# Low parts of weights in three stages of a two-block transformer: every subtraction on VectorE instead of every second one on GpSimd

## Chip, cores and metric

One NeuronCore of a Trainium2 chip runs the whole program. The metric is device time in microseconds (us). Engines carry the names of the profile: PE is TensorE's matmul, PEld its weight load, DVE is VectorE, ACT is ScalarE, POOL is GpSimd, SP is SyncE, which issues most of the DMAs.

## What is computed

Two blocks of two layers each, in float32, on 512 tokens of width 1024, and 256 context tokens in the second block. The second block is the one that the change touches:

```python
for i in range(DEPTH):                                   # second_block
    hx = rmsnorm(x, norm_g[i, 0]) * (1.0 + sc_x) + sh_x
    hc = rmsnorm(ctx, norm_g[i, 0]) * (1.0 + sc_c) + sh_c
    if i % N_MIXERS == 0:
        yx = conv_module(hx, *cp)                        # and yc for ctx
    else:
        yx, yc = attention_module(hx, hc, ...)           # 16 heads of 64, 4 key heads
    x = x + g_x * rmsnorm(yx, norm_g[i, 1])
    fx = rmsnorm(x, norm_g[i, 2]) * (1.0 + scf_x) + shf_x
    x = x + gf_x * rmsnorm(swiglu(fx, ffn_w1[i], ffn_w3[i], ffn_w2[i]), norm_g[i, 3])
    # the same for ctx where i < DEPTH - 1

def conv_module(h, ...):
    a, gt = jnp.split(h @ w_pw1 + b_pw1, 2, axis=-1)
    u = a * jax.nn.sigmoid(gt)
    u = depthwise_conv(u, w_dw) + b_dw                   # 31 taps
    return jax.nn.silu(layernorm(u, ln_g, ln_b)) @ w_pw2 + b_pw2
```

## The kernel before, in words

Every matrix product runs in three passes, so that float32 weights and activations keep their precision: each operand is split into a high part (rounded to the matmul's format) and a low part (what is left), and PE adds high x high, high x low and low x high (`dense`, L184 to L186; `dense_tok`, L192 to L194). Activations are split where they are made (L269, L270, L282, L284, L285). Weights come from memory in float32, chunk by chunk, and are split on the fly by `Core.weights`: SP loads a chunk of at most 128x1024 into `raw`, ACT casts it into `whi` (L165), and DVE or POOL subtracts, `wlo = raw - whi` (L168). `raw`, `whi` and `wlo` have three buffers each. Which engine subtracts is set by one number, `core.lo_pool`: 0 means always DVE, 2 means that every second chunk (by a running count) goes to POOL, 1 means always POOL. The two lines that say so:

```python
eng = nc.gpsimd if self.lo_pool and self.chunks % self.lo_pool == 0 else nc.vector
eng.tensor_tensor(lo[:, :n], raw[:, :n], hi[:, :n], op=ALU.subtract)
```

The program sets that number stage by stage. In the second block: `conv_layer` takes `CONV_LO` (2) for the products of the gated unit (`glu`, 32 chunks) and for the second product on the context (`back(T)`, 8 chunks); `ffn2` takes 2 in its first and its last part, which this text calls the edges of the feed-forward, and 0 between; `attention_layer` takes `PROJ_LO` (2) for the queries', keys' and values' projections (`project`, 28 chunks); the attention's output product uses 1, then `LO_O` (2), and is not touched. The first block has settings of its own, not touched either.

Around these products the engines have other work. In the convolution, DVE runs the 31 taps over the context, one instruction per tap (L929, tile `yc`), as side work behind the gated unit; POOL builds tap weights (L936, `wt`) and issues half of the copies of shifted channels (L941, `ug`); PE runs the taps over x (L948, `cv`). At the edges of the feed-forward and after the attention, norms run from one part to the next: sums of squares (L221, `acc`), a column sum on PE (L238), an inverse root by Newton steps on DVE (L204 to L210, `rs_*`), its broadcast on PE (L243), scaling of eight tiles, three of them on ACT and POOL (L258, L259) and five on DVE (L261), the residual sum (L830, three on POOL, five on DVE) and the split (L269, L270). In the projections DVE turns queries and keys (L1082, `rp`), POOL finishes that (L1084, L1085) and subtracts low parts of activations (L1119, L1133, `stk`), and PE transposes them (L1091, `qT`).

The order on each engine is set when the program is built: a scheduler takes ready instructions by their place in the program and by an estimate of their length, and each engine then runs its list strictly in that order. So an instruction that moves to another engine changes the lists of both, and the scheduler rearranges PE's and ACT's too.

Of the kernel before, what the change touches and what calls it, by code (L numbers as in the profile page):

```python
# [17 lines left out]
PSUM = bass.MemoryType.PSUM  # L18
# [10 lines left out]
# ---------------------------------------------------------------- column vectors  # L29
# [38 lines left out]
PROJ_LO = 2  # L68
MM = 4
AT = 4  # L70
CONV_LO = 2
# [15 lines left out]
class Scratch:  # L87
    """[128, 256] tiles that the norms pass through"""
# [8 lines left out]
class Core:  # L97
    """Pools, constants and the pieces that every layer uses."""
# [25 lines left out]
    def issue_behind(self, ins, others):  # L124
        """keep ins behind the others in their engine's queue"""
        for o in others:
            self.tc.add_manual_dep(ins.ins, o.ins.name,
                                   mybir.DependencyInfo(mybir.DependencyClass.NoSync, mybir.DependencyReason.DATA),
                                   reason="activation tables")
        return ins  # L130
# [15 lines left out]
    def side_work(self, n):  # L146
        """up to n steps of work that runs beside the matrix products"""
        for _ in range(n):
            if next(self.side, None) is None:
                return  # L150
# [7 lines left out]
    # ---- weights: raw float32 in, exact hi + lo parts out  # L158
# [12 lines left out]
    def chunk(self, src):  # L171
        """one chunk [128, k, n] of a matrix"""
        _, k, n = src.shape
        hi, lo = self.weights(src.rearrange("p k n -> p (k n)"), k * n)
        return (hi[:, : k * n].rearrange("p (k n) -> p k n", n=n),
                lo[:, : k * n].rearrange("p (k n) -> p k n", n=n))

    def dense(self, out, w, xs, cols=slice(0, S)):
        """out[feature, token] = sum over k of w[k].T @ xs[k], in three exact-product passes"""
        hi, lo = w  # L180
        mm = self.nc.tensor.matmul
        n = len(xs)
        for k, (xh, xl) in enumerate(xs):
            mm(out, lhsT=hi[:, k, :], rhs=xh[:, cols], start=(k == 0), stop=False)  # L184
            mm(out, lhsT=hi[:, k, :], rhs=xl[:, cols], start=False, stop=False)  # L185
            mm(out, lhsT=lo[:, k, :], rhs=xh[:, cols], start=False, stop=(k == n - 1))  # L186

    def dense_tok(self, out, x, cols, w, first, last):
        """out[token, feature] += x.T @ w for one tile of k and 128 tokens"""
        (xh, xl), (wh, wl) = x, w  # L190
        mm = self.nc.tensor.matmul
        mm(out, lhsT=xh[:, cols], rhs=wh, start=first, stop=False)  # L192
        mm(out, lhsT=xh[:, cols], rhs=wl, start=False, stop=False)
        mm(out, lhsT=xl[:, cols], rhs=wh, start=False, stop=last)  # L194

    # ---- rsqrt on a small tile, by Newton steps on the vector engine
# [16 lines left out]
    # ---- norms over the features of a feature-major array  # L213
    def square_sum(self, pool, sums, x, k):
        """the squares of tile k join sums, which ends as two tiles"""
        nc = self.nc
        n = x.shape[-1]
        sq = pool.tile("sqx" if k else "acc")[:, :n]
        nc.scalar.activation(sq, x, AF.Square)
        if 0 < k < KD - 1:  # L220
            nc.vector.tensor_tensor(sums[0], sums[0], sq, op=ALU.add)  # L221
        else:
            sums.append(sq)

    def rstd_psum(self, sums):
        """1 / rms per token on all partitions, in PSUM; and the last step of the rsqrt"""
        nc = self.nc
        n = sums[0].shape[-1]
# [17 lines left out]
    def rstd(self, pool, sums):  # L246
        """the same in PSUM and in SBUF"""
        pb, _ = self.rstd_psum(sums)
        rb = pool.tile("rb")[:, : pb.shape[-1]]
        self.nc.scalar.copy(rb, pb)  # L250
        return pb, rb

    def times_rb(self, pool, x, scale, rb, k):
        """x * rb * scale"""
# [9 lines left out]
    def modulate(self, pool, out, x, scale, shift, rb, k):  # L264
        """out (hi, lo) = x * rb * scale + shift"""
        nc = self.nc
        hi, lo = out
# [4 lines left out]
    def modulated(self, pool, h, xs, cols, scale, shift, sums):  # L272
        """the norm of the tiles xs, scaled and shifted per feature, into the columns of h"""
# [17 lines left out]
    # ---- modulation vectors: w.T tile by tile against rows of the activation, summed on the fly  # L291
    def modulation_rows(self, wt, vecs, bias, dsts, tiles, first=0, pool=None):
        """one step per tile of 128 outputs; wt: [48, 128, 1024]"""
# [21 lines left out]
    def silu_row(self, pool, src, name):  # L315
        """silu of a vector of 1024, on all partitions"""
# [6 lines left out]
    def gains(self, g, mod, slot, name):  # L323
        """g * (1 + mod[slot]) as columns"""
# [5 lines left out]
# ------------------------------------------------------------------------------- first block  # L330
def rope_tables(core, pool, cos, sin):
    """cos and sin of positions * inv_freq, token-major [128, 4, 32]"""
# [26 lines left out]
def rope_gains(core, pool, cos, sin, g, name):  # L359
    """cos and sin with the gains of both halves folded in: [128, 4, 4, 32]"""  # L360
# [9 lines left out]
def mla_latents(core, l, ts):  # L370
    """the products of the latents and of the shared rope key, token-major"""
# [11 lines left out]
def mla_heads(core, tmp, pool, kp, l, ups, cos, sin, rows):  # L383
    """queries, keys and values of all heads; kp holds what the attention reads"""
# [47 lines left out]
    def rope(eng, out, x, tab, shape):  # L432
        """out, x: views [..., 64]; tab: (cos g1, sin g2, cos g2, sin g1) broadcast to the shape"""
# [6 lines left out]
    # queries: token-major, then turned; the rope halves of a pair of heads share a tile of keys,  # L440
    # so each head's queries are zero in the other head's rows
# [34 lines left out]
    # keys and values  # L476
# [42 lines left out]
def mla_attention(core, pool, yp, heads, table):  # L519
    """causal softmax attention; y as hi and lo parts, one pair of tiles per head"""  # L520
# [41 lines left out]
def stick_rows(core, kp, l, which):  # L562
    """queries (which = 0) or keys (1) of the stick-breaking heads, feature-major"""
# [39 lines left out]
def stick_attention(core, pool, yp, heads, table):  # L603
    """a = exp(z + reverse cumulative sum of log(1 - sigmoid z)) over the past keys; keys on partitions"""
# [36 lines left out]
def gate(core, parts, l, br, m):  # L641
    """the argument of a gate's sigmoid, in tiles that hold a part of the tokens each"""
# [11 lines left out]
def gated(core, l, parts, ys, br, m, behind):  # L654
    """sigmoid(g) * (y @ w_branch) for one tile of features, in place of g"""
# [11 lines left out]
def first_layer(core, pool, l, ups, mod, cos, sin, next_mod, early, finish):  # L667
    """the layer's normed input is in core.h already; finish(columns, sums) makes the next one's"""
# [57 lines left out]
    with tc.tile_pool(name=f"ff{l}", reuse_waits="tile", bufs=1) as fp:  # L726
        tails = {}

        def up(i, hl, cols):
            """one tile of the hidden layer; a causal convolution of width 3 sits before the gate"""  # L730
# [57 lines left out]
# ------------------------------------------------------------------------------ second block  # L788
class Base:
    """the tokens of x or of ctx, feature-major: x, the normed input h (hi, lo) and a layer's output y"""  # L790
# [5 lines left out]
class Stream:  # L796
    """some columns of a base that go through a phase together"""
# [23 lines left out]
def post_norm(core, st, gate_slot, ng, squares=True):  # L821
    """x += gate * rmsnorm(y, ng); leaves the sums of squares of the new x"""
# [17 lines left out]
def ffn2(core, fp, i, bases, parts, nbuf, finish):  # L840
    """swiglu as a sequence of steps; parts: (first tile, end, steps up or down of streams that share the
    weights); streams run one after the other hide each other's norms"""
    nc, a = core.nc, core.a
    for part, (k0, k1, steps) in enumerate(parts):
        first, last = part == 0, part == len(parts) - 1
        hid = {b.tag: [core.pair(fp, b.n, "hid" + b.tag, nbuf) for _ in range(k0, k1)] for b in bases}
        core.lo_pool = 2 if first or last else 0
# [38 lines left out]
def conv_layer(core, X, A, B, T, post, pre, between):  # L886
    """conformer convolution module of x (as one stream X, then its halves A and B) and of ctx (T)"""
# [3 lines left out]
    with tc.tile_pool(name="cv_c", reuse_waits="tile", bufs=1, side="right") as cp, ExitStack() as es:  # L891
# [12 lines left out]
        def glu(st, m, u):  # L904
            """u = (h @ w_a + b_a) * sigmoid(h @ w_g + b_g) for one tile of channels, with zeros around"""
# [12 lines left out]
        def taps_dve(us):  # L918
            """the convolution over ctx on the vector engine, one step per tap"""
# [12 lines left out]
        def shifted(m, u):  # L932
            """over x on the tensor engine: four shifted copies of each 32 channels fill the rows of the array"""
# [25 lines left out]
        def layer_norm(st, t):  # L959
            """silu(layernorm) into h; t: the sum of all tiles but the last"""  # L960
# [63 lines left out]
def axial_tables(core, pool):  # L1024
    """cos and sin with the queries' and the keys' gains folded in, and the gains; pool's one tile holds them
    until the attention's probabilities take its place"""
# [16 lines left out]
def attention_layer(core, pool, A, B, T, axial, tables, dense_psum, finish):  # L1043
    """grouped-query attention of x (halves A and B) over x and ctx (T); 16 heads of 64, 4 key heads"""
# [3 lines left out]
    with ExitStack() as es:  # L1048
# [8 lines left out]
        with tc.tile_pool(name="at_t", reuse_waits="tile", bufs=1) as tmp:  # L1057
# [18 lines left out]
            def rope(out, x, tab, t, heads):  # L1076
                """interleaved pairs: out, x [128, heads, 64] views"""
# [9 lines left out]
            def turned(src, dst, act):  # L1087
                """four tiles [128 tokens, 128] turned into dst [128, 4, 128]"""
# [8 lines left out]
            def keys(st, pss):  # L1097
                """for the queries' hi and lo parts stacked on the partitions: each part of the keys twice"""
# [55 lines left out]
        with tc.tile_pool(name="at_p", reuse_waits="tile", bufs=1) as pp, core.psum_pool("ps_a") as pa:  # L1154
            pairs = []

            def scores(u):
                """of 128 queries of a head, and the negated maximum of each"""
# [13 lines left out]
            def exponentials(u, ps, s2, rc):  # L1172
                """turned to put the keys on the partitions"""
# [27 lines left out]
            def output(p, yps):  # L1201
                """divided by the sums of the exponentials, into h"""
# [268 lines left out]
# --------------------------------------------------------------------------------- the host  # L1471
def _mt(w):
    """[..., K, M] -> [..., M / 128, 128, K / 128, 128]: one contiguous chunk per 128 columns"""
# [6 lines left out]
def _kc(w, kk):  # L1480
    """[..., K, N] -> [..., K / (128 kk), 128, kk, N]"""
# [6 lines left out]
def _col(v):  # L1488
    """[..., n * 128] -> [128, prod * n] columns, tile by tile"""
    return v.reshape(-1, P).T  # L1490


def _pairs(a, b):
    """interleave chunk lists along the chunk axis"""
# [78 lines left out]
```

## Time and profile before

| | before |
|---|---|
| time, median of 3 runs | 3262.71 us (3258.6 to 3264.51) |
| span of the profiled execution, first to last instruction | 3256.1 us |
| own time of the profiled execution | not listed apart from its span; the median lies 6.6 us above the span |
| PE busy | 3045.2 us, 94% of the span |
| DVE busy | 2118.7 us, 65% |
| ACT busy | 1378.8 us, 42% |
| POOL busy | 818.3 us, 25% |
| mean granted TensorE clock | 0.972 |
| L168 on POOL | 189 instructions, mean 2472 ns |
| L168 on DVE | 433 instructions, mean 1163 ns |

Busy shares are means over stages with different limits. The convolution lies at about 1562 to 1822 us from the start of the span, the first edge of the feed-forward behind it up to 2000, its middle up to 2400, its last edge to 2500, the projections to 2640, the attention to some 2820, the last feed-forward from 2845 to the end, with edges up to 2905 and from 3190. A stage is best read from a view that gives each engine's busy time in that stretch.

### The profile page before, as it was taken

Reading aid. Unit: us, or ns where it says so; the run is one execution under the profiler, and the core shown is the slowest. Engines: PE = TensorE matmul, PEld = TensorE weight load, DVE = VectorE, ACT = ScalarE, POOL = GpSimd, SP = SyncE. Lnnn points to the kernel's source line nnn. Section 1 sums busy time; section 2 is a strip of 40 time slices with the busy share of each in tenths; the row PEclk is TensorE's granted clock in tenths of the full one; section 3 lists DMA queues with packets and bytes.
Section 4 is the critical chain, followed back from the end, with each engine's and each line's share of the span. In section 5 each row is a group of like instructions: output and inputs, shape, how many; then the busy total and the mean of one; then the engine's idle time right before and its main releaser. Section 6 shows DMA issues by size and latency. Waiting matters only on the chain. (4 is left out here: it accounts for less than half of the span.)

```text
span 3256.1 us, 45125 instructions
## 1 busy us (share of the span) xinstructions
PE 3045.2 (94%) x16916; PEld 2554.5 (78%) x16916; DVE 2118.7 (65%) x3863; ACT 1378.8 (42%) x2523; POOL 818.3 (25%) x618
## 2 busy tenths in 40 slices
PE   6999999999999999999899789999998789999997
PEld 5776888888777787877856589888887667898887
DVE  7654775657543688888997786544549976672326
ACT  4535552335534562324513564222235556553223
POOL 4000223233000222223555352000025621240023
PEclk9999999999999999999999889999999989999998
DMA  6442445654221355554434345333434310243323
GB/s 239 135 138 95 136 168 190 192 179 150 90 72 49 123 174 175 170 188 131 146 111 119 104 136 175 98 110 130 138 106 139 119 44 14 75 143 111 94 97 117
DMA packets 129322, 416.69 MB, mean 128 GB/s; under 512 B 16208, under 2 KB 21840, under 8 KB 129104
## 3 DMA queue, kind: packets, MB, share of 16 engines
q1 hardware_dynamic: 123984, 404.96, 38.5%
q10 hardware_dynamic: 3072, 4.43, 0.5%
q0 software_dynamic: 2048, 4.43, 0.5%
q8 instruction: 133, 2.18, 0.3%
q14 instruction: 85, 0.70, 0.1%
HBM read 402.81 MB, written 2.10 MB: 124 GB/s over the span
## 5 line engine op out<-in xcount | busy, mean ns | idle before, releaser
L165 ACT CAST whi<-raw 128x1024 fp32r<-128x1024 f32 (+4 forms) x622 | 599.0, 966 | 1008.8 <-PE dn L185 299.9
L168 POOL TENSOR_TENSOR wlo<-raw,whi 128x1024 fp32r<-128x1024 f32 (+3 forms) x189 | 467.0, 2472 | 1275.0 <-ACT whi L165 1237.4
L168 DVE TENSOR_TENSOR wlo<-raw,whi 128x1024 fp32r<-128x1024 f32 (+4 forms) x433 | 503.2, 1163 | 284.3 <-ACT whi L165 276.8
L184 PE MATMUL dn<-hi,whi 128*128 128x256 f32 (+1 forms) x1088 | 363.5, 338 | 19.8 <-DVE x L778 13.5
L186 PE MATMUL dn<-hi,wlo 128*128 128x256 f32 (+1 forms) x1088 | 361.5, 336 | 7.6 <-DVE wlo L168 7.5
L185 PE MATMUL dn<-lo,whi 128*128 128x256 f32 (+1 forms) x1088 | 364.5, 336 | 1.7 <-DVE lo L285 1.5
L184 PE MATMUL up<-hh,whi 128*128 128x512 f32 (+1 forms) x800 | 292.1, 367 | 7.2 <-ACT hh L269 7.2
L185 PE MATMUL up<-hl,whi 128*128 128x512 f32 (+1 forms) x800 | 292.5, 366 | 0.3 <-DVE hl L270 0.2
L186 PE MATMUL up<-hh,wlo 128*128 128x512 f32 (+1 forms) x800 | 291.7, 365 | 0.0
L308 DVE SCALAR_TENSOR_TENSOR mjunk<-mraw,crow 128x1024 f32<-128x1024 f32 (+1 forms) x176 | 224.0, 1273 | 39.9 <-PE g L185 21.1
L184 PEld LDWEIGHTS dn<-hi,whi 128*128 128x128 f32 x1088 | 207.3, 191 | 47.9 <-issue 14.0
L186 PEld LDWEIGHTS dn<-hi,wlo 128*128 128x128 f32 x1088 | 206.9, 191 | 32.5 <-DVE wlo L168 9.9
L185 PEld LDWEIGHTS dn<-lo,whi 128*128 128x128 f32 x1088 | 208.8, 192 | 25.0 <-DVE lo L285 2.3
L860 DVE TENSOR_TENSOR s<-s,pv 128x512 f32<-128x512 f32 (+1 forms) x76 | 41.0, 539 | 283.7 <-PE pv L186 278.0
L184 PE MATMUL pa<-hh,whi 128*128 128x512 f32 (+1 forms) x496 | 179.5, 362 | 6.2 <-ACT whi L165 3.4
L185 PE MATMUL pa<-hl,whi 128*128 128x512 f32 (+1 forms) x496 | 178.8, 361 | 2.8 <-DVE hl L270 2.7
L186 PE MATMUL pa<-hh,wlo 128*128 128x512 f32 (+1 forms) x496 | 178.0, 359 | 2.0 <-DVE wlo L168 2.0
L184 PEld LDWEIGHTS up<-hh,whi 128*128 128x128 f32 x800 | 152.4, 191 | 31.4 <-ACT hh L269 7.7
L185 PEld LDWEIGHTS up<-hl,whi 128*128 128x128 f32 x800 | 152.4, 191 | 24.5 <-DVE hl L270 0.8
L186 PEld LDWEIGHTS up<-hh,wlo 128*128 128x128 f32 x800 | 152.3, 191 | 23.8
L186 PE MATMUL pv<-hh,wlo 128*128 128x512 f32 (+1 forms) x432 | 152.7, 353 | 0.2 <-POOL wlo L168 0.2
L184 PE MATMUL pv<-hh,whi 128*128 128x512 f32 (+1 forms) x432 | 152.5, 353 | 0.0
(471 smaller groups left out, 7427.7 us busy)
## 6 DMA issues: line engine op xcount, KB each, us to landing
raw<-in_w SPq DMA_DIRECT2D x148, 512.0 KB, 3.4
raw<-in_w_up SPq DMA_DIRECT2D x100, 512.0 KB, 3.5
mraw<-in_w_modt SPq DMA_DIRECT2D x96, 512.0 KB, 3.6
mraw<-in_w_adat SPq DMA_DIRECT2D x80, 512.0 KB, 3.4
raw<-in_w_pw SPq DMA_DIRECT2D x56, 512.0 KB, 3.5
raw<-in_w_down SPq DMA_DIRECT2D x48, 448.0 KB, 3.5
raw<-in_w_g SPq DMA_DIRECT2D x32, 512.0 KB, 3.2
raw<-in_w_out SPq DMA_DIRECT2D x32, 512.0 KB, 3.6
```

The costliest lines, as they stand in the source:

```text
L165: nc.scalar.copy(hi[:, :n], raw[:, :n])
L168: eng.tensor_tensor(lo[:, :n], raw[:, :n], hi[:, :n], op=ALU.subtract)
L184: mm(out, lhsT=hi[:, k, :], rhs=xh[:, cols], start=(k == 0), stop=False)
L185: mm(out, lhsT=hi[:, k, :], rhs=xl[:, cols], start=False, stop=False)
L186: mm(out, lhsT=lo[:, k, :], rhs=xh[:, cols], start=False, stop=(k == n - 1))
L308: behind(nc.vector.scalar_tensor_tensor(junk, raw, 1.0, v, op0=ALU.mult, op1=ALU.mult, accum_out=d[:, f : f + 1]))
L860: nc.vector.tensor_tensor(s, s, pv, op=ALU.mult)
```

## The change

Three settings go from 2 to 0; `core.chunks` counts on as before. The rest of the diff takes out comments and docstrings.

```diff
-PROJ_LO = 2
+PROJ_LO = 0
 MM = 4
 AT = 4
-CONV_LO = 2
+CONV_LO = 0
...
 def ffn2(core, fp, i, bases, parts, nbuf, finish):
...
-        core.lo_pool = 2 if first or last else 0
+        core.lo_pool = 0
```

Over the program, L168 stands 189 times on POOL and 433 times on DVE before, and 79 and 543 times in the change: 110 subtractions move, 90 of 128x1024, 16 of 128x512 and 4 of 128x768.

POOL's list in the projections, before (`stk` are low parts of queries and keys that PE waits to transpose, `qf` and `kt` turned queries and keys, `ctx` and `hp` the context's norm):

```order
L830 TENSOR_TENSOR ctx_10741<-ctx_10741,hp 128x256
L168 TENSOR_TENSOR wlo<-raw,whi 128x1024
L830 TENSOR_TENSOR ctx_10743<-ctx_10743,hp 128x256
L1084 TENSOR_TENSOR kt_23103<-rp 128x128
L1085 TENSOR_TENSOR kt_23103<-rp 128x128
L168 TENSOR_TENSOR wlo<-raw,whi 128x1024 x2
L1133 TENSOR_TENSOR stk<-qf,stk 128x8x64
```

The same place of POOL's list in the change:

```order
L830 TENSOR_TENSOR ctx_10741<-ctx_10741,hp 128x256
L259 TENSOR_TENSOR hp<-hp,rb 128x256
L830 TENSOR_TENSOR ctx_10743<-ctx_10743,hp 128x256
L1133 TENSOR_TENSOR stk<-qf,stk 128x8x64
L1084 TENSOR_TENSOR kt_23129<-rp 128x128
L1085 TENSOR_TENSOR kt_23129<-rp 128x128
L1133 TENSOR_TENSOR stk<-qf,stk 128x8x64
```

Three subtractions stood between the context's residual sums and the next `stk`; none is left.

DVE's list at the context's residual sums in the same stage (`pg` is a gain, `rs_v` begins the inverse root that waits for the sums `acc`), before:

```order
L830 TENSOR_TENSOR ctx_10740<-ctx_10740,hp 128x256
L830 TENSOR_TENSOR ctx_10742<-ctx_10742,hp 128x256
L168 TENSOR_TENSOR wlo<-raw,whi 128x1024
L261 SCALAR_TENSOR_TENSOR hp<-yc_13721,pg,rb 128x256
L261 SCALAR_TENSOR_TENSOR hp<-yc_13722,pg,rb 128x256
L830 TENSOR_TENSOR ctx_10744<-ctx_10744,hp 128x256
L830 TENSOR_TENSOR ctx_10745<-ctx_10745,hp 128x256
```

And in the change:

```order
L261 SCALAR_TENSOR_TENSOR hp<-yc_13722,pg,rb 128x256
L168 TENSOR_TENSOR wlo<-raw,whi 128x1024
L830 TENSOR_TENSOR ctx_10744<-ctx_10744,hp 128x256
L221 TENSOR_TENSOR acc<-acc,sqx 128x256
L830 TENSOR_TENSOR ctx_10745<-ctx_10745,hp 128x256
L825 TENSOR_TENSOR pg<-mod_105,cols 128x8
L168 TENSOR_TENSOR wlo<-raw,whi 128x1024
L221 TENSOR_TENSOR acc<-acc,sqx 128x256
L168 TENSOR_TENSOR wlo<-raw,whi 128x1024
L221 TENSOR_TENSOR acc<-acc,sqx 128x256 x3
L168 TENSOR_TENSOR wlo<-raw,whi 128x1024 x2
L240 TENSOR_SCALAR rs_v<-rb 128x2
```

From the first of the residual sums (`ctx_10738`) to `rs_v` DVE has three subtractions in its list before and six in the change.

## Rows read from the trace of the kernel before

**Rows 1.** Busy time of each engine by stretch (stretch, its length, engines, PEclk, DMA, GB/s).

```profile
1562.00:1740.00 178.00, 160.05 (x950) 117.69 (x948) 169.87 (x309) 51.52 (x73) 98.36 (x94) 0.94 0.40 121
1740.00:1822.00 82.00, 79.96 (x564) 51.51 (x563) 44.57 (x83) 33.78 (x60) 33.53 (x37) 1.00 0.43 127
1822.00:2000.00 178.00, 145.95 (x1069) 140.87 (x1069) 144.37 (x312) 107.98 (x221) 76.51 (x53) 0.87 0.40 127
2000.00:2400.00 400.00, 400.00 (x2280) 351.02 (x2279) 191.57 (x309) 91.32 (x146) 12.56 (x6) 1.00 0.39 126
2400.00:2500.00 100.00, 89.37 (x599) 81.61 (x598) 75.33 (x149) 48.61 (x100) 42.05 (x32) 0.95 0.37 111
2500.00:2640.00 140.00, 107.88 (x495) 84.49 (x494) 133.31 (x268) 73.03 (x126) 85.36 (x64) 0.90 0.37 122
2845.00:2905.00 60.00, 53.46 (x394) 51.99 (x393) 51.90 (x109) 37.18 (x74) 27.77 (x19) 0.90 0.42 140
2905.00:3190.00 285.00, 285.00 (x1378) 239.48 (x1377) 80.56 (x93) 84.53 (x112) 40.91 (x18) 1.00 0.34 107
3190.00:3257.00 67.00, 47.32 (x390) 46.35 (x388) 46.38 (x82) 22.68 (x37) 27.69 (x19) 0.86 0.38 118
```

**Rows 2.** The same stretches, L168 alone: DVE busy (count), POOL busy (count).

```profile
1562.00:1740.00 178.00, 18.20 (x15) 57.30 (x15) 0.94 0.40 121
1740.00:1822.00 82.00, 9.90 (x7) 15.16 (x6) 1.00 0.43 127
1822.00:2000.00 178.00, 23.98 (x20) 48.28 (x20) 0.87 0.40 127
2400.00:2500.00 100.00, 16.07 (x17) 28.64 (x17) 0.95 0.37 111
2500.00:2640.00 140.00, 26.70 (x17) 35.74 (x14) 0.90 0.37 122
2845.00:2905.00 60.00, 10.40 (x8) 17.38 (x7) 0.90 0.42 140
3190.00:3257.00 67.00, 11.26 (x7) 17.29 (x7) 0.86 0.38 118
```

**Rows 3.** Timeline, 1890 to 1902 us, of DVE (start, length, instruction, idle before).

```profile
1890.66 1.22 DVE L168 TENSOR_TENSOR wlo<-raw,whi 128x1024 fp32r<-128x1024 f32 x1
1891.80 0.42 DVE L221 TENSOR_TENSOR acc<-acc,sqx 128x256 f32<-128x256 f32 x1
1893.15 1.92 DVE L221 TENSOR_TENSOR acc<-acc,sqx 128x256 f32<-128x256 f32 x1 [0.93 <-ACT sqx L219]
1895.49 1.23 DVE L168 TENSOR_TENSOR wlo<-raw,whi 128x1024 fp32r<-128x1024 f32 x1 [0.43 <-ACT whi L165]
...
1901.02 1.23 DVE L168 TENSOR_TENSOR wlo<-raw,whi 128x1024 fp32r<-128x1024 f32 x1 [0.20 <-ACT whi L165]
```

**Rows 4.** Timeline of POOL in the same time.

```profile
1892.38 2.40 POOL L168 TENSOR_TENSOR wlo<-raw,whi 128x1024 fp32r<-128x1024 f32 x1 [2.44 <-ACT whi L165]
```

**Rows 5.** Timeline of DVE, its first and last stretched instruction in these stretches.

```profile
1564.00 2.44 DVE L270 SCALAR_TENSOR_TENSOR hl<-hp,modx,hh 128x256 fp32r<-128x256 f32 x1
...
3228.89 3.38 DVE L168 TENSOR_TENSOR wlo<-raw,whi 128x1024 fp32r<-128x1024 f32 x1
```

**Rows 6.** Timeline of the projections at 2532 us: POOL, DVE and PE.

```profile
2531.73 2.52 POOL L168 TENSOR_TENSOR wlo<-raw,whi 128x1024 fp32r<-128x1024 f32 x1
...
2531.98 3.37 DVE L168 TENSOR_TENSOR wlo<-raw,whi 128x1024 fp32r<-128x1024 f32 x1
...
2535.40 0.79 PE L193 MATMUL pj<-wlo,hh 128*128 128x512 f32 x1 [3.83 <-DVE wlo L168]
```

**Rows 7.** Waits of PE, 2500 to 2640 us (total, times, longest).

```profile
PE pj L193 <- DVE wlo L168: 10.8, 7, 3.8
PE qT L1091 <- POOL stk L1119: 5.9, 3, 5.0
```

**Rows 8.** Costliest groups, the page: L168 on DVE (busy, mean; idle before, releaser).

```profile
L168 DVE TENSOR_TENSOR wlo<-raw,whi 128x1024 fp32r<-128x1024 f32 (+4 forms) x433 | 503.2, 1163 | 284.3 <-ACT whi L165 276.8
```

## The prediction

> **What bounds the kernel now.** I read first the busy time of the engines by stretch [rows 1], because the 94% of PE over the whole span hides two kinds of stage. In the middle of each feed-forward (2000 to 2400 and 2905 to 3190 us) PE is busy without a gap, 400.00 of 400 and 285.00 of 285 us, while DVE works 191.57 and 80.56 us: PE alone bounds these. Everywhere else that the change reaches, PE has gaps and DVE is nearly full: 169.87 of 178 us in the convolution, 133.31 of 140 in the projections, 144.37 of 178 at the first edge. The gaps of PE in these stretches (length less busy) are 18, 2, 32, 11, 32, 7 and 20 us, 122 in all; more than that the change can't win, except by the clock, which the rows give as 0.86 to 1.00 there. So the question is whether DVE gets more or less to do in the stretches with gaps.
>
> Next I read how the subtractions are spread over these stretches [rows 2]. POOL does 15, 6, 20, 17, 14, 7 and 7 of them, 86 in all; the other 24 of the 110 that move lie in the two stretches where PE has no gap. One takes POOL 2.4 us (48.28 / 20), and 3.8 in the convolution (57.30 / 15).
>
> Last the timeline, for what a subtraction on POOL does to DVE. At 1892.38 POOL begins one of 2.40 us [rows 4]. The sum of squares that DVE begins at 1893.15 lasts 1.92 us and ends with it, where the same instruction at 1891.80 lasts 0.42 [rows 3]. DVE is held for 1.5 us by work that was given to POOL to spare it. It's the pattern of all these stretches: the first case is a split at 1564.00, 2.44 us long, and the last a subtraction of DVE's own at 3228.89, 3.38 us where others take 1.22 [rows 3, 5]. I went through the timeline of the seven stretches, took each DVE instruction that overlaps a POOL subtraction (and no other POOL instruction for longer), and counted its length above the shortest usual one of its form. 73 instructions are held by over 0.3 us, and the sum by stretch is 27.4, 8.6, 25.0, 17.2, 26.2, 10.2 and 12.8 us, **127 us** in all, or 1.48 per subtraction. At 2532 us one sees it reach PE: POOL subtracts from 2531.73, DVE's own subtraction from 2531.98 then takes 3.37 us, and PE stands for 3.83 us until it has this low part [rows 6].
>
> **What the change adds and removes.** It removes 110 subtractions from POOL and adds them to DVE. On DVE one of 128x1024 costs the time from its start to the next instruction's, 1891.80 - 1890.66 = 1.14 us [rows 3]; for 128x512 I take 0.61, about half (an estimate from that row; 13 of the 86 are of that size). By stretch that adds 17.0, 6.8, 22.2, 13.0, 15.9, 7.9 and 7.9 us, **91 us**. Against the 127 that go, DVE has 36 us less to do: -10.4, -1.8, -2.8, -4.2, -10.3, -2.3 and -4.9. The 24 subtractions in the full stretches add some 26 us to DVE, which lie beside PE and cost nothing; if PE were not full there, they would cost up to 26.
>
> How much of it is time? It depends on the wait that ends last in each stretch, and I choose a share for each:
> - Convolution, -10.4: DVE's surplus is the taps over the context, which PE wants only at their end, so I take half, **-5**; the cap is PE's gap of 18.
> - 1740 to 1822, PE at 79.96 of 82: 0.
> - First edge, -2.8: chains of norms, each behind the other, **-2**.
> - Last edge, -4.2: **-3**.
> - Projections, -10.3: DVE is full and PE waits 10.8 us for low parts of DVE [rows 1, 7]; **-8**. Also, three POOL subtractions less stand before a `stk` that PE waits for (the list in the change); PE waits 5.9 us for such tiles [rows 7]. I leave that as a reserve.
> - First edge of the last feed-forward, -2.3: **-1**. Its last edge, -4.9, a chain that ends the program: **-3**.
>
> Together -22.
>
> **The wait that is added.** A subtraction on DVE can't start before ACT's cast, and DVE's list stands behind it; on POOL only POOL stood. What it costs isn't seen for the moved ones, so I bound it. From below 0: two of the four subtractions between 1885 and 1902 don't wait. From above the page's mean over all subtractions on DVE, 284.3 / 433 = 0.66 us [rows 8], 57 us for 86; most of that idle time belongs to stages in which DVE has nothing else. I take what DVE shows where it is busy: 0, 0, 0.43 and 0.20 us at these four [rows 3], 0.16 each. For the 80 outside 1740 to 1822 that makes 13 us, and half of it on the path, **+6**. Where several subtractions stand together in a chain, as between the context's residual sums and the inverse root (six instead of three), three times 1.14 = 3.4 us are put into this chain; they are part of the 91.
>
> Sum: -22 + 6 = **-16 us**. Against the span of 3256.1 us that is 3240; the median of the runs lies 6.6 us above the span, so the forecast is 3262.7 - 16 = **3247 us**. A difference of under 0.2%, 6.5 us, can't be told from none by a measurement of this kernel.
>
> **Rivals.**
> *No change.* DVE is relieved, but not where PE waits: at 1893 us, for example, the held sum of squares was ahead of its need, since DVE idles before the next ones [rows 3]. For it speaks that much of the 127 us may be such slack; against it that 133.31 of 140 us in the projections leave none. The gains of the edges vanish, the 8 of the projections stay, the added wait takes 6: 3261. Chance 0.18.
>
> *Slower, by DVE waiting for casts.* DVE's list now holds every subtraction, and each that is early stops the chain of norms behind it until ACT has cast and, behind that, until PE has freed a buffer. The balance tips where the moved subtractions wait more than 36 / 86 = 0.42 us each. With the page's mean of 0.66 [rows 8] they wait 57 us, 21 more than DVE wins: 3283. For it: six subtractions in one chain where there were three, and a scheduler that sets this order by estimates. Against it: the rows of a busy DVE show 0.16. Chance 0.15.
>
> *Slower, because a full DVE gets more work.* If the held instructions were late for some other reason and POOL's subtractions were free for DVE, the added work would stand alone: 169.87 + 17.0 = 187 us in a stretch of 178 and 133.31 + 15.9 = 149 in one of 140, 9 us each; the other stretches have room. That is +18, 3281. The stretched instructions that end with the POOL instruction speak against it [rows 3 to 6]. Chance 0.05. The Trainium skill (Perfetto Trace Analysis, "Optimizing Scalar/DVE Operations") says that work may sensibly be moved off a saturated DVE to ScalarE or even to GpSimd, which by itself is this rival and speaks against the change. It adds that between DVE and GpSimd this may not help, since the two share a port; the trace agrees with this second half, 1.92 us for an instruction of 0.42.
>
> That the change doesn't do what it says is excluded by the lists: 110 subtractions leave POOL's.
>
> **How the numbers follow.** The forecast's case, a gain between 7 and 41 us, has 0.62. Its far end is the whole relief outside 1740 to 1822 (10.4 + 2.8 + 4.2 + 10.3 + 2.3 + 4.9 = 35) with no added wait and 5.9 us of PE's waits for `stk`: 3262.7 - 41 = 3222. At the other side the range takes in no change and half of the two slower cases, to **3272**; what lies above, and a gain of more than 41, is under 2 in 10. So 3222 to 3272, faster 0.62, the same 0.18, slower 0.15 + 0.05 = 0.20.
>
> **What would show it.** In the profile of the changed kernel: L168 on POOL 79 times; DVE instructions of the projections and edges back at their usual lengths (L221 near 0.42 us, L168 near 1.22); DVE busy in the projections about 10 us lower although it has 14 more subtractions; PE's waits for low parts and for `stk` there down from 10.8 and 5.9. The forecast is wrong if DVE's idle time before L168 for ACT's casts grows by more than 36 us in these stretches, or if the gaps of PE stay where they are while DVE's are new.

## The result, and the profile after

| | before | after |
|---|---|---|
| median of 4 runs | 3260.65 us (3255.70 to 3264.51) | 3204.69 us (3202.73 to 3209.26) |
| span of the profiled execution | 3256.1 us | 3203.2 us |
| mean granted clock | 0.972 | 0.976 |

The change is faster: ratio 0.9832, 95% interval 0.9818 to 0.9846, that is 56 us where 16 were forecast. The time lies below the range. Of all runs below, one, at a mean granted clock of 0.573, took 4893.98 us; it is left out of its kernel's median.

The page of the profile after, the engines' busy time and the two groups of L168 (the first answers to [rows 8]):

```profile
PE 3026.3 (94%) x16916; PEld 2541.2 (79%) x16916; DVE 2094.5 (65%) x3973; ACT 1378.0 (43%) x2521; POOL 556.8 (17%) x508
...
L168 DVE TENSOR_TENSOR wlo<-raw,whi 128x1024 fp32r<-128x1024 f32 (+4 forms) x543 | 620.9, 1145 | 366.0 <-ACT whi L165 357.6
...
L168 POOL TENSOR_TENSOR wlo<-raw,whi 128x1024 fp32r<-128x1024 f32 (+1 forms) x79 | 194.1, 2458 | 391.9 <-ACT whi L165 388.7
```

PE's busy time fell by 18.9 us (from 3045.2) with the same 16916 products, and DVE's by 24.2 (from 2118.7) with 110 instructions more. To see where, I cut both traces at the same products of PE: convolution, first edge, last edge, projections, output product of the attention with the first edge of the last feed-forward, its last edge. Busy time by stretch, before (columns as in [rows 1]):

```profile
1563.70:1822.20 258.50, 239.19 (x1504) 168.38 (x1504) 212.74 (x387) 83.69 (x129) 131.70 (x128) 0.96 0.41 124
1822.20:1995.20 173.00, 140.95 (x1042) 136.71 (x1042) 139.60 (x303) 106.58 (x218) 76.51 (x53) 0.86 0.39 123
2377.80:2500.70 122.90, 112.27 (x704) 100.71 (x703) 80.35 (x156) 55.18 (x108) 47.35 (x35) 0.96 0.37 112
2500.70:2634.60 133.90, 104.20 (x481) 81.32 (x479) 129.88 (x262) 69.49 (x120) 85.36 (x64) 0.91 0.38 126
2821.60:2935.80 114.20, 104.56 (x812) 102.84 (x811) 81.48 (x156) 64.24 (x122) 53.84 (x34) 0.94 0.43 139
3188.10:3239.20 51.10, 47.42 (x395) 47.01 (x394) 39.68 (x59) 22.18 (x34) 22.97 (x13) 0.97 0.45 142
```

The same stretches after:

```profile
1565.00:1798.30 233.30, 229.75 (x1505) 161.76 (x1505) 197.01 (x409) 82.99 (x128) 69.48 (x98) 1.00 0.45 137
1798.30:1963.70 165.40, 139.91 (x1046) 135.99 (x1043) 135.85 (x324) 105.83 (x218) 29.47 (x33) 0.87 0.40 130
2346.20:2458.30 112.10, 105.45 (x695) 95.23 (x693) 72.99 (x163) 53.33 (x102) 13.30 (x15) 1.00 0.39 118
2458.30:2587.40 129.10, 106.14 (x490) 84.98 (x489) 121.94 (x288) 72.72 (x128) 49.92 (x51) 0.89 0.41 135
2775.00:2887.60 112.60, 103.66 (x813) 101.81 (x812) 84.71 (x169) 64.20 (x123) 22.59 (x21) 0.94 0.44 141
3139.90:3186.80 46.90, 46.17 (x396) 46.00 (x394) 35.62 (x67) 21.78 (x34) 4.65 (x6) 1.00 0.47 147
```

The lengths fall by 25.2, 7.6, 10.8, 4.8, 1.6 and 4.2 us, 54.2 in all. Each of the stretches between and around these six agrees within 1.4 us in the two traces. Of the 54.2, PE's gaps (length less busy) give 36.7, and PE's busy time the other 17.5, 9.4 of it in the convolution and 4.9 in the last edge and the projections together (nine products changed sides of that cut). In the convolution and the last edge the granted clock rises from 0.96, a mean between its levels, to the upper one of 2.4 GHz throughout; in the first edge (0.86, then 0.87) and the projections (0.91, then 0.89), where PE still has 25 and 23 us of gaps, it doesn't rise. DVE is busy for 35.6 us less in these stretches (683.74 to 648.11), near the relief of 36 that the prediction worked out; that the gaps of PE fell by about as much is not by itself a proof that they follow it, as a run below shows.

The taps over the context in the convolution (busy, mean ns, idle before), before and then after:

```profile
L929 DVE SCALAR_TENSOR_TENSOR yc<-uc,wdv,yc 128x256 f32<-128x256 f32 x240 | 127.6, 598 | 0.7 <-ACT yc L927 0.7
...
L929 DVE SCALAR_TENSOR_TENSOR yc<-uc,wdv,yc 128x256 f32<-128x256 f32 x240 | 102.7, 491 | 0.1
```

The same 240 instructions take 24.9 us less. The waits of PE in the convolution (us in total, times, longest), before:

```profile
PE cv L948 <- DMA ug<-u: 6.7, 2, 3.7
PE pa L184 <- DVE uc L915: 5.2, 2, 3.6
PE pg L184 <- ACT whi L165: 2.1, 3, 1.0
PE mu L963 <- DVE totc L957: 2.0, 1, 2.0
PE pg L186 <- POOL wlo L168: 1.6, 1, 1.6
```

And after:

```profile
PE pg L186 <- DVE wlo L168: 1.0, 2, 0.8
PE rb L243 <- DVE rs_y L210: 0.9, 1, 0.9
PE cv L948 <- DMA ug<-u: 0.9, 1, 0.9
PE pa L184 <- DVE uc L915: 0.8, 1, 0.8
```

Both large ones are read in the timeline of before (start, length, instruction, idle before):

```profile
1605.82 4.18 DVE L929 SCALAR_TENSOR_TENSOR yc<-uc,wdv,yc 128x256 f32<-128x256 f32 x5
1606.65 2.67 POOL L168 TENSOR_TENSOR wlo<-raw,whi 128x1024 fp32r<-128x1024 f32 x1 [2.62 <-ACT whi L165]
1609.92 1.21 DVE L168 TENSOR_TENSOR wlo<-raw,whi 128x1024 fp32r<-128x1024 f32 x1
1611.46 0.47 DVE L915 SCALAR_TENSOR_TENSOR uc<-pa,cols,sg 128x256 f32<-128x256 f32 x1
1611.98 0.58 PE L184 MATMUL pa<-ctx_hl,whi 128*128 128x256 f32 x1 [3.60 <-DVE uc L915]
...
1658.77 15.13 DVE L929 SCALAR_TENSOR_TENSOR yc<-uc,wdv,yc 128x256 f32<-128x256 f32 x38
1665.07 11.08 POOL L168 TENSOR_TENSOR wlo<-raw,whi 128x1024 fp32r<-128x1024 f32 x1 [7.47 <-ACT whi L165]
1676.10 3.93 POOL L941 DMA_DIRECT2D ug<-u  x8
1681.46 1.06 PE L948 MATMUL cv<-ug,wt 128*32 128x512 f32 x2 [3.71 <-DMA ug<-u]
```

In the first, five taps take 4.18 us, about 2 of them held by POOL's subtraction, and `uc`, for which PE waits, stands behind them in DVE's list. In the second it is the other way round: DVE runs 38 taps without a pause, and POOL's subtraction, begun 6.3 us into this run, lasts 11.08 us instead of 2.40 and ends 2.2 us after the last tap, as if it had only then begun (the expectation for the copies below counts 27 taps, those that end after 1663.5). The copies of shifted channels stand behind it in POOL's list, and PE waits 3.71 us for them. The prediction had the number, 57.30 / 15 = 3.8 us per subtraction [rows 2], and didn't ask why it wasn't 2.4.

### The profile page after: what moved, and what is told of

Its sections match the earlier page's. It is cut to its first block, busy times and chain, and to the rows that moved or that the text cites. A ratio compares the mean times of both kernels' runs of the same rounds, so it can differ in the third digit from the quotient of the medians.

```text
span 3203.2 us, 45064 instructions
## 1 busy us (share of the span) xinstructions
PE 3026.3 (94%) x16916; PEld 2541.2 (79%) x16916; DVE 2094.5 (65%) x3973; ACT 1378.0 (43%) x2521; POOL 556.8 (17%) x508
## 4 chain that ended last, share of the span: by engine, by line
PE 42%; DVE 7%; ACT 1%; DMA 1%; issue 1%; POOL 0%; ACTq 0%; DVEq 0%; POOLq 0%
PE pa L185 4%; PE pa L184 4%; PE pa L186 4%; PE pv L186 3%; PE pv L184 3%; PE pv L185 3%; PE dn L186 3%; PE dn L184 3%; PE dn L185 3%; PE cv L948 2%; PE yps L1198 2%; DVE wlo L168 1%; DVE hp L261 1%; PE pT L1187 1%; PE sc L1165 1%
## 5 line engine op out<-in xcount | busy, mean ns | idle before, releaser
L168 DVE TENSOR_TENSOR wlo<-raw,whi 128x1024 fp32r<-128x1024 f32 (+4 forms) x543 | 620.9, 1145 | 366.0 <-ACT whi L165 357.6
L259 POOL TENSOR_TENSOR hp<-hp,rb 128x256 f32<-128x256 f32 x90 | 76.5, 862 | 1151.0 <-ACT hp L258 1136.6
L168 POOL TENSOR_TENSOR wlo<-raw,whi 128x1024 fp32r<-128x1024 f32 (+1 forms) x79 | 194.1, 2458 | 391.9 <-ACT whi L165 388.7
L186 PEld LDWEIGHTS dn<-hi,wlo 128*128 128x128 f32 x1088 | 205.2, 189 | 28.2 <-DVE wlo L168 5.5
```

Source lines behind the costliest of these rows:

```text
L259: nc.gpsimd.tensor_tensor(p, p, rb[1], op=ALU.mult)
```

## The experiments

**Each setting alone.** The three edits, each on the kernel before:

```diff
-CONV_LO = 2
+CONV_LO = 0
...
-        core.lo_pool = 2 if first or last else 0
+        core.lo_pool = 0
...
-PROJ_LO = 2
+PROJ_LO = 0
```

The convolution: 

> The convolution's setting alone. Theory (a subtraction on POOL holds DVE; in the convolution this delays what PE waits for, so the stage wins far more than DVE's own balance): the convolution is 25.3 us shorter as in the full change (258.7 to about 233 us), its matmuls run at a granted clock near 1.00, and the rest stays: 3260.7 - 25 = 3235 us. Rival 1 (my forecast's shares): -5 us, 3256 us, and the rest of the 56 us comes from elsewhere. Rival 2 (the stage gains only together with the edge behind it, because the scheduler's order of the two changes): somewhere between, 3245 us, with the convolution at some 245 us.

The edges: 

> The feed-forward's edges alone. Theory (each stage's gain is its own): the first edge -7.9, the last edge -10.7, first edge of the last feed-forward -1.8, its last edge -5.4, together -25.8: 3235 us. Rival 1 (my forecast's shares, 2 + 3 + 1 + 3): -9, 3252 us. Rival 2 (what the edges showed came from the stages before them, which handed over earlier): within 5 us of before, 3256 to 3261 us.

The projections: 

> The projections' setting alone. Theory (each stage's gain is its own): -4.9 us, 3256 us, with the projections at 129 us instead of 134 and DVE busy about 8 us less in them. Rival 1 (my forecast's share): -8, 3253 us. Rival 2 (the gain of 4.9 us came with the other stages): within 2 us of before.

Against 3260.81 us for the kernel before they took 3238.11 (0.9926, 0.9911 to 0.9941), 3234.13 (0.9918, 0.9903 to 0.9933) and 3253.89 us (0.9975, 0.9966 to 0.9985): 22.7, 26.7 and 6.9 us less, together 56.3, the whole of the change. Stage by stage in the profiled executions (us, against before, cut at the same products):

| | convolution | first edge | last edge | projections | output, first edge | last edge |
|---|---|---|---|---|---|---|
| the change | -25.2 | -7.6 | -10.8 | -4.8 | -1.6 | -4.2 |
| convolution alone | -24.4 | +0.1 | -1.3 | -0.2 | +1.5 | -0.9 |
| edges alone | +0.4 | -9.3 | -11.3 | +2.2 | -2.8 | -4.2 |
| projections alone | +6.0 | -2.1 | -0.6 | -10.6 | +4.7 | 0.0 |
| repeated subtractions | +10.1 | +13.4 | +5.7 | +11.5 | +11.2 | +0.7 |
| fills | -21.6 | -3.8 | -1.3 | -8.0 | -3.4 | -4.2 |

The settings of the convolution and of the edges alone win about what the change wins in their stages, and the three times add up; in stages that an edit leaves alone single traces differ by up to 6 us. So each stage's gain is its own, and the forecast's shares fail for the convolution and the edges. The projections alone won 10.6 us in their own stage, more than expected, but that execution lost 6.0 in the convolution, whose settings this edit leaves alone. The timeline there:

```profile
1658.10 15.13 DVE L929 SCALAR_TENSOR_TENSOR yc<-uc,wdv,yc 128x256 f32<-128x256 f32 x38
...
1662.07 13.38 POOL L168 TENSOR_TENSOR wlo<-raw,whi 128x1024 fp32r<-128x1024 f32 x1 [5.15 <-ACT whi L165]
1675.38 3.93 POOL L941 DMA_DIRECT2D ug<-u  x8
```

The subtraction lasted 13.38 us instead of 11.08 beside the same run of 38 taps, because it began 4.0 us into it instead of 6.3; it ends 2.2 us after the last tap again. How long the two engines stop each other depends on when each begins. PE then waited 9.17 us for the copies instead of 3.71. These 5.5 us more don't come from the longer subtraction: POOL's subtraction ended 0.7 us earlier in this trace than before, PE came to the copies 3.0 us earlier, and the copy that released it landed 6.9 us after its issue instead of 3.8.

**Is it the hold, or POOL's lateness?** Three kernels give POOL work again beside the full change, for every second chunk, after DVE's subtraction, with a result that nobody reads:

```diff
+        if self.spare and self.chunks % self.spare == 0:
+            self.idle_work(raw, hi, n)
...
+    def idle_work(self, raw, hi, n):
+        self.nc.gpsimd.tensor_tensor(raw[:, :n], raw[:, :n], hi[:, :n], op=ALU.subtract)
```

In the second the body is a copy of two columns and two fills; in the third one copy of the whole chunk:

```diff
+        self.nc.gpsimd.tensor_copy(raw[:, :2], hi[:, :2].bitcast(F32))
+        for v in (0.0, 1.0):
+            self.nc.gpsimd.memset(raw[:, :n], v)
...
+        self.nc.gpsimd.tensor_copy(raw[:, :n], hi[:, :n].bitcast(F32))
```

The subtractions: 

> The full change; in addition, for every second chunk of the three stages, POOL subtracts whi from raw once more, after DVE and in place, and nobody reads the result. So no product waits for POOL's result, and DVE does every low part. Theory (POOL's subtraction holds DVE while it runs): the DVE instructions beside it are stretched again by some 1.5 us for each of the 110, DVE carries both the subtractions and the holds, and most of the 56 us is given back: 3245 to 3290 us, the convolution at 250 us or more. Rival (the low parts simply came late from POOL, 2.4 us instead of 1.2 and at the end of POOL's own list, and PE waited for them): nobody waits for these, so the time stays at 3203 to 3215 us.

The fills: 

> The full change; in addition, for the same chunks, POOL copies two columns of whi into raw and then fills raw twice with a constant (two fills of 128x1024, by a row of 0.53 us for 128x512 about 1.06 us each, so POOL is busy for 2.1 us a chunk, nearly as with the subtraction, and raw is kept as long). Theory (what holds DVE is that POOL reads two operands while it runs): fills read nothing, DVE's instructions keep their usual lengths, and the time stays at 3203 to 3215 us. Rival 1 (what cost the time is that POOL's list was full, so that tap weights, copies and residual sums behind it came late, or that raw came free late): it is given back with the fills as with the subtractions, 3240 us or more. Rival 2 (any work of POOL holds DVE): the same time as with the subtractions, and stretched DVE instructions beside the fills.

The copies: 

> As the run with the repeated subtractions, but POOL copies whi into raw, in one instruction of the chunk's size with one operand, where it subtracted. Theory (POOL holds DVE while it reads SBUF, with one operand as with two): DVE's instructions beside the copies are stretched by what is left of the copy when they begin; with copies about half as long as the subtractions (an estimate; two fills were 1.91) the cost is about half of the 109 us between the run with the subtractions and the full change: 3240 to 3270 us. Rival (only POOL's two-operand subtraction holds DVE): the same as with the fills, 3208 to 3220 us.

They took 3313.74 (1.0166, 1.0150 to 1.0181), 3214.42 (0.9862, 0.9848 to 0.9877) and 3242.87 us (0.9944, 0.9924 to 0.9964): 109, 10 and 38 us above the change (the copies in two runs, the others in four). The subtractions cost more than expected, 3313.74 us where 3290 was the upper end: DVE carries the low parts and the holds. With the subtractions, the page's engines, the group of POOL's subtractions, and the timeline at 1604 us (the edit adds lines: L937 is the tap, L175 the added work):

```profile
PE 3058.1 (92%) x16916; PEld 2562.3 (77%) x16916; DVE 2238.4 (68%) x3973; ACT 1379.0 (42%) x2521; POOL 810.9 (24%) x618
...
L175 POOL TENSOR_TENSOR raw<-raw,whi 128x1024 f32<-128x1024 f32 x90 | 224.7, 2497 | 854.8 <-DVE wlo L169 439.9 <-DMA raw<-in_w 356.8 <-issue 20.4
...
1604.07 2.55 POOL L175 TENSOR_TENSOR raw<-raw,whi 128x1024 f32<-128x1024 f32 x1 [5.00 <-DVE wlo L169]
1604.31 2.60 DVE L937 SCALAR_TENSOR_TENSOR yc<-uc,wdv,yc 128x256 f32<-128x256 f32 x1
1606.91 0.47 DVE L937 SCALAR_TENSOR_TENSOR yc<-uc,wdv,yc 128x256 f32<-128x256 f32 x1
```

With the fills (L939 is the tap):

```profile
PE 3030.7 (94%) x16916; PEld 2551.5 (79%) x16916; DVE 2102.1 (65%) x3973; ACT 1378.5 (43%) x2521; POOL 784.7 (24%) x838
...
L177 POOL MEMSET raw<- 128x1024 f32 x180 | 171.8, 955 | 9.5
...
1606.86 1.97 POOL L177 MEMSET raw<- 128x1024 f32 x2
1607.87 0.87 DVE L939 SCALAR_TENSOR_TENSOR yc<-uc,wdv,yc 128x256 f32<-128x256 f32 x2
```

With the copies:

```profile
PE 3040.1 (94%) x16916; PEld 2552.1 (79%) x16916; DVE 2132.2 (66%) x3973; ACT 1377.1 (42%) x2521; POOL 672.0 (21%) x618
...
L175 POOL COPY raw<-whi 128x1024 f32<-128x1024 f32 x90 | 102.6, 1141 | 892.6 <-DVE wlo L169 481.6 <-DMA raw<-in_w 359.1 <-issue 19.8
```

DVE's list has 3973 instructions in all three, as in the change, where it is busy for 2094.5 us. The subtractions add 143.9 us to it (1.31 each), the fills 7.6 (0.07 a chunk) although POOL is busy nearly as long (784.7 against 810.9), the copies 37.7 (0.34). So POOL's full list and the buffer that is kept longer (by fills of 1.91 us a chunk, where a subtraction takes 2.50) account for some 10 us, and nobody waited for the results: it is shown that POOL's reading beside DVE costs the rest. What POOL's lateness itself cost before can be read too: in the six stretches PE waited 4.3 us for low parts of POOL and 23.4 us for low parts of DVE; after the change it waits 0 and 10.0. The copy cost less than the half expected of the 109; it was inside the range.

The Trainium skill (SBUF — State Buffer, "Who interferes with whom") says that a DVE instruction with two inputs in SBUF contends with a GpSimd instruction that reads SBUF, not with one that only writes it, and that the one which comes second is blocked. The trace agrees: 2.60 us for a tap beside a subtraction, 0.87 for two beside a fill, and 11.08 for a subtraction beside taps. In the last case it was a run of 38 taps that kept the subtraction from ending, and not one instruction alone.

**The rest of POOL's subtractions on DVE too.**

```diff
-LO_O = 2
+LO_O = 0
...
-                core.lo_pool = 2
+                core.lo_pool = 0
...
-                    core.lo_pool = 1
+                    core.lo_pool = 0
```

> The full change and, beyond it, the last 79 subtractions of POOL (70 in the first block, 9 around the attention) on DVE too. Theory (a held DVE costs where PE has gaps): POOL's remaining 79 hold DVE by some 76 us in the changed kernel, but PE is busy 382.6 of 390 and 400.0 of 425 us in the two stretches of the first block, so at most 7 + 25 us are to be had there and the attention's 9 give 1 to 3: 3190 to 3202 us. Rival 1 (the first block's DVE is near full, 359 of 425 us, and 70 more subtractions of 1.14 us make it the bound): slower than the full change, 3210 to 3230 us. Rival 2 (no difference, POOL's subtractions there hold instructions that nobody waits for): 3202 to 3208 us.

3178.01 us, 0.9742 (0.9727 to 0.9756) of before, 27 us below the change and below the range expected. Busy time of the first block's last stretch, before and then in this kernel:

```profile
1140.00:1563.70 423.70, 399.00 (x2096) 341.42 (x2095) 358.92 (x551) 178.66 (x276) 127.28 (x75) 0.97 0.52 168
```

```profile
1137.50:1539.70 402.20, 392.84 (x2095) 337.13 (x2095) 348.96 (x585) 178.41 (x276) 48.83 (x37) 0.99 0.56 177
```

The stretch is 21.5 us shorter, and DVE has 10 us less to do in it with 35 subtractions more (53 to 88): a DVE busy for 85% of the stretch was no reason to leave work on POOL. This is the best kernel of the study.

**And POOL's norm tiles?** On top of the last kernel:

```diff
-POOL_TILES = (1, 3, 5)
+POOL_TILES = ()
```

> The kernel with all subtractions on DVE, and in addition no norm tile on POOL: the scaling (L259) and the residual sums (L830) that POOL did for three of eight tiles go to DVE, the scaling with its ACT part. Theory (the hold is worth removing only where it is longer than the work that moves): in the kernel with all subtractions on DVE, L259 and L830 hold DVE by 20.7 + 12.8 = 34 us in 245 instructions, that is 0.14 each beside a length of some 0.4 us on DVE, so DVE gets more work than it is relieved of, mostly in the chains of norms: 0 to 25 us slower than 3178 us. Rival (every work of POOL is better on DVE): 5 to 15 us faster.

3201.30 us, 0.9820 (0.9804 to 0.9837): 23 us slower than with them on POOL, as the theory had it. Its 0.14 us is the hold for each of the 245 DVE instructions beside them; for each of the 120 instructions that leave POOL (90 of L259, 30 of L830) the 34 us are 0.28, to be set against some 0.45 on DVE. DVE, which takes over ACT's part of the scaling too, is busy for 8.1 us more (2106.9, then 2115.0). Not everything is better on DVE; that the hold against the work that moves decides it is the reading of this one run.

**Is DVE's time the bound in the convolution?** On the kernel before:

```diff
-                for j in (15,) + tuple(j for j in range(31) if j != 15):
+                for j in (15,) + tuple(j for j in range(31) if j not in (0, 10, 15, 20)):
```

> The kernel before with three of the 31 taps over the context left out in each of eight tiles: 24 instructions of L929 less, at the 0.598 us that one takes there 14.4 us less for DVE in the convolution; no subtraction moves and POOL's work is untouched. Theory (DVE, busy 95% there, is the bound of the convolution, and each us taken from it shortens the stage, with the higher clock that PE gets when it stands less on top): the convolution shortens by 14 us or more, with PE's idle time down by about 10 and PE's busy time by some 4 to 9 us: 3247 us or less. Rival 1 (my forecast's half: the taps over the context are surplus that is wanted at their end only): -7, 3254 us. Rival 2 (only the holds of particular instructions matter): within 3 us of before.

3257.56 us, 0.9996 (0.9986 to 1.0006): no difference. DVE is busy for 195.80 us in the convolution instead of 212.74, more relief than the change brings there (15.7), and the stage is 4.3 us shorter in the profiled execution. The first theory fell. PE's largest waits stand as they were:

```profile
PE cv L948 <- DMA ug<-u: 6.8, 3, 3.5
PE pa L184 <- DVE uc L915: 5.2, 2, 3.6
```

So DVE's sum of work alone doesn't set the stage; what is left is which instructions are held and who stands behind them.

**The context's half alone.** Of the gated unit's chunks, the first 16:

```diff
-        core.lo_pool = CONV_LO
+        core.lo_pool = 0
...
             core.side_work(CONV_C)
+        core.lo_pool = CONV_LO
```

> The kernel before with the subtractions of the gated unit's first half alone, the 16 chunks for the context, all on DVE: 8 of the convolution's 21 move. Theory (a hold costs where an instruction that PE waits for stands behind it in DVE's list, and PE's gaps show where that is): of PE's gaps in the convolution before, 0.95, 1.60, 3.60 and 1.62 us lie in this half (1580 to 1630 us), the two of 2.96 and 3.71 us behind it; these 7.8 us go, and PE's higher clock adds 2 to 5: -9 to -13 us, 3248 to 3252 us, with the gaps for the copied channels left. Rival 1 (the gain is spread as the instructions are): 8 of 21 of 24 us, -9, so it is told apart by the gaps that stay, not by the time. Rival 2 (the whole of the convolution's 24 us starts in this half, since what is late there stays late): -20 or more, 3241 us or less.

3248.99 us against 3258.97 (0.9965, 0.9949 to 0.9981): 10 us, as expected. The profiled execution was the fastest of them, 3243.42 us, and its convolution is 15.7 us shorter. But the waits for `ug`, which the theory had left standing, went with those for `uc`, and others came:

```profile
PE mu L963 <- DVE totc L957: 3.9, 1, 3.9
PE pg L186 <- POOL wlo L168: 3.5, 2, 2.1
```

**The copies away from POOL.** On the kernel before:

```diff
-UG_LAST = 2
+UG_LAST = 4
...
-UG_ACT = 2
+UG_ACT = 4
```

> The kernel before with all sixteen copies of shifted channels per tile (L941, ug) issued by ACT, where POOL issued eight of them; all subtractions as before. Theory (the hold works both ways: one subtraction of POOL lasted 11.08 us beside a run of 27 taps on DVE, the copies stood behind it in POOL's list and PE waited 3.71 us for them): PE's two gaps for ug, 2.96 and 3.71 us, go, the gap of 3.60 us for uc stays, since it comes from a held tap on DVE; the time falls by 6.7 us and 1 to 4 by the clock: 3249 to 3253 us. Rival (the copies were late because u itself was late, or the eight issues more delay ACT's casts by as much): the gaps for ug stay or come back as waits for whi, 3257 to 3265 us.

3268.55 us, 1.0022 (1.0012 to 1.0032): slower, and by more than the rival's 3265. The waits for the copies fell only from 6.7 to 4.9 us, those for `uc` stood at 5.2, and PE waited longer for casts on ACT (4.0 us in the convolution, 2.1 before), for low parts of POOL (3.8, 1.6 before) and for sums of squares (3.7, 1.5 before):

```profile
PE cv L948 <- DMA ug<-u: 4.9, 5, 1.7
PE pw L184 <- ACT whi L165: 2.2, 3, 1.4
```

How the convolution's 25 us divide between held DVE instructions and held subtractions of POOL with the copies behind them stays open: without the first eight of POOL's subtractions both waits went, and with the copies away from POOL both stayed for the most part.

## Why the prediction was wrong in size

- *What bounds, and the hold.* Right. The sums of squares (L221) of the convolution are back at a mean of 419 ns from 783, and the repeated subtractions show the cause. That the relief of DVE came out at 35.6 us for 36 is in part luck: by stage it was 15.7 for 12.2 in the convolution, 3.7 for 2.8, 7.4 for 4.2, 7.9 for 10.3, 3.2 more work instead of 2.3 less at the output with the first edge of the last feed-forward, and 4.1 for 4.9; these stretches hold 95 of the subtractions, the prediction's 86. Over the program DVE was busy for 24.2 us less, where the prediction's 36 - 26 make 10.
- *"Convolution, -10.4: DVE's surplus is the taps over the context, which PE wants only at their end, so I take half, -5."* This step failed first: -25.2, of which 15.8 are PE's gaps (19.3 to 3.5). That the taps are surplus was right, as the run without 24 of them shows. But the work that PE does want (`uc`, the copies) stands between the taps in the same lists. A hold there is not paid for by slack elsewhere.
- *"More than that the change can't win, except by the clock."* The clock was named and got no term. PE's busy time on the same products fell by 17.5 us in the six stretches, 9.4 of it in the convolution. The prediction's own rows had it: granted clock of 0.94 and 0.95 in the two stretches [rows 1] that now run at 1.00.
- *Edges and the end.* -2, -3, -1 and -3 forecast, -7.6, -10.8, -1.6 and -4.2 measured, some 5 of the second by the clock. The first edge's gaps fell by 6.6 us, more than the 3.75 by which DVE was busy less there.
- *Projections, -8.* -4.8 in the change's execution, -10.6 in the run of this edit alone: the size of the term stands, PE's waits for low parts of DVE there fell from 10.8 to 2.0 us, and the reserve for `stk` did not come (8.9 us for such tiles in both, 5.9 and 3.0, then 3.6 and 5.3).
- *"+6" for the added wait.* DVE's idle time before L168 for casts grew much more than thought, from 28.2 to 81.2 us in the six stretches, 0.56 for each of the 95 that moved there, near the 0.66 of the rival that forecast 3283 us. PE's waits for those low parts fell all the same, from 23.4 to 10.0 us; whether the casts cost it something further down a chain isn't shown (it waits 8.7 us for ACT's `hh`, 2.8 before). In the last edge, after:

```profile
DVE wlo L168 <- ACT whi L165: 21.0, 11, 4.1
DVE s L860 <- PE pv L186: 14.4, 5, 4.1
```

  Before, these were 3.1 and 34.0: DVE waits for a cast where it waited for a product. That the forecast is wrong if this idle time grows by more than 36 us was a wrong test; a wait must be followed to PE before it is priced.

In hindsight, the six shares at their full relief (35) without the added wait and PE's busy time (17.5) add up to 52. That is bookkeeping and no mechanism: the run without 24 taps relieved DVE by 16.9 us in the convolution and won nothing.

## What to carry to other kernels

Price an offload to GpSimd by both engines' instructions that are stretched while it reads, and look for a duration above its usual one on either side: here 1.3 us of DVE were lost for each subtraction that DVE itself does in 1.14. Then weigh a hold not by DVE's busy time but by what PE waits for behind it in the same list, and add what PE's clock gives back where its gaps close, as it did here in the convolution and the last edge. Work that only writes, or whose hold is shorter than the work itself (0.28 us against some 0.45 for a norm tile), may stay.

## What was not expected of the hardware

The hold works both ways, and a run of DVE instructions holds POOL for longer than one of them: 11.08 and 13.38 us for a subtraction of 2.40 beside taps of 0.47 us each that followed one another without a pause. After the change POOL's tap weights (L936) take 6.84 us at 1668.80, where the one at 1680.05 before took 1.93. Fills of the same size held DVE for almost nothing.
